# Norms with whole rows in freed buffers, low halves split by VectorE, and turned operands in a one-bank PSUM ring

## The chip, the cores and the metric

One core of a Trainium2 chip runs the whole kernel. The metric is the device time of one execution in microseconds (us), as the median of several runs. Five engines have instruction streams of their own: TensorE (PE, with its weight loads PEld), VectorE (DVE), ScalarE (ACT), GpSimd (POOL) and SyncE (SP), which here only issues transfers; "SPq" and "ACTq" are the queues of transfers that SyncE and ScalarE issue.

## What is computed

One decoder layer on x of 2048 tokens by 1024 features, all in float32:

```python
hn = rms_norm(h, mix_pre_g)
proj = hn @ w_in                       # q (512), k (128), v (128), conv input u (1024)
attn_out = sliding_window_attention(q, k, v, attn_sinks, rel_bias)   # window 128, 8 heads
conv_out = conformer_conv(u, ...)      # GLU, 31 causal taps, LayerNorm, silu, @ w_conv_pw
mixed = concatenate([attn_out, conv_out]) @ w_out
h = h + rms_norm(mixed, mix_post_g)
hn = rms_norm(h, ffn_pre_g)
f = (silu(hn @ w_gate) * (hn @ w_up)) @ w_down      # d_ff 2816
h = h + rms_norm(f, ffn_post_g)
```

The change concerns the two norms in the middle (behind `mixed` and ahead of the feed-forward products), and some splits of weights.

## The kernel before, in words

A float32 product is made of three matmuls: each operand is split into a high half (ScalarE's rounding copy, L127 for weights) and a low half (the difference, L129 for weights, by GpSimd if `on_pool`, else by VectorE). VectorE's operations go through the helpers `stt`, `vtt` and `vts`, so most of them show as L94, and TensorE's products as L85. The names in the profile are tile@stage: `w@A` is a weight tile of stage A. Tiles live in rings, where a new tile waits for the last reader of the tile that had the buffer before. The rings that matter here have in SBUF x 4, wx 1, gb 2, hl 8, ql 4, chl 5, mid 4, fa 4, at 2, fc 3, raw 2 and w 6 buffers, and in PSUM (banks of 128x512) mm 4, tr 3 and ct 1.

The tokens go in four tiles of 512. The stages are:

- A: the input projection of a tile. Its weights are loaded as raw@A (L137), or their low halves as w@A<-lo_in (L126) where an earlier tile has made them. A turned v goes over fa@A (copied by ScalarE, L398, then transposed, L407).
- B: sliding-window attention, in the tr ring, with masks on GpSimd (`affine_select`, L494).
- C: the convolution. Its 31 taps are multiply-adds of VectorE (fc@C<-glu@C,colt,fc@C) that run at a low priority beside everything up to about 1300 us; its tail transposes in the ct ring (L549, L601) and writes mixT to DRAM.
- U: `stage_fold` (L611) multiplies w_conv_pw into the convolution's half of w_out once, ahead of W0. Its splits are 4 in the ring mid and 8 in chl, and their 12 low halves are made by GpSimd.
- W0 to W3: `stage_w` (L706), the output projection of one tile. Its activations are loaded from mixT (L717), split (L719), and multiplied into the accumulators x@W (W0) or mid@W. W0 makes the low halves of w_out's attention rows (8, on GpSimd) and stores them; W1 to W3 load them.
- `norm_w` (L759), called N0 to N3 here, behind each W: the rows of the post-norm are loaded as two halves gb@W (L697); sums of squares by ScalarE (L765); an inverse root (`rsqrt`, L145 to L156, whose refinements are on GpSimd for W0 to W2); the accumulators are scaled as eight halves; x is loaded in part whole in wx (L778) and in part as halves in fa or at (L784), and added (L779, L785: for W0 the tile in wx and two halves on GpSimd, the others on VectorE; for W1 to W3 all on VectorE); the sum is stored to h_scr (L786), its squares are summed (L787), a second inverse root follows, and the scaled rows go to hn_scr.
- H: the feed-forward input is read back from hn_scr by columns and turned (`turned`, L827, in tr), scaled (L847), split and kept as operands. The first pair of tiles (H0) and the second pair (H2) are apart.
- F: the gate and up products (with raw@F loads at L914, kept partial sums gb@F<-keeps at L921, put into banks by ScalarE at L936), for two tiles at a time. G: the down projection, which reads fa@G<-mids (L1146), mb@G<-td (L1150), copies p@G (L1218) into banks (L1219). TS makes sums of w_down beforehand.

Stages are generators that yield a cost. Main stages run in a fixed sequence; the others sit in lanes (L1290 on) that are advanced by the main stage's yielded cost times a rate, so that a changed yield moves instructions of other stages too. A scheduler then fixes one order of instructions for each engine. Within an engine (and in SyncE's queue of transfers) an instruction that waits holds all that stand behind it.

The lines of `norm_w` that the prediction speaks of, cut:

```python
gb = load_gb(0)                                   # two halves in gb
...
post_scale(acc[s], gb, r[:, s : s + 1])           # two stt of 512 columns
...
(vtt if w in WV or w == 0 and s % 2 else ptt)(acc[s][:, cs], xt, acc[s][:, cs], ALU.add)
```

Of the kernel before, what the change touches and what calls it, by code (L numbers as in the profile page):

```python
# [37 lines left out]
def layer_kernel(ctx, tc, x, xT, cols, rows, sinks, relb, onehot, w_in, w_pw, w_out, w_gate, w_up, w_down, out):  # L38
# [572 lines left out]
    def stage_fold():  # L611
# [8 lines left out]
        for i in range(2):  # L620
            lab[0] = "U0"
            raw = two(w_pw[2 * i : 2 * i + 2].rearrange("c p t -> p c t"))
            wp += [split_w(raw[:, j], "mid") for j in range(2)]
            yield 2.76
        for n in range(2):
            wo = []
            for i in range(2):
                lab[0] = "U0"
                c = 4 + 2 * i
                raw = two(w_out[c : c + 2, :, n * T : (n + 1) * T].rearrange("c p t -> p c t"))  # L630
                wo += [split_w(raw[:, j], "chl") for j in range(2)]
                yield 0.1 if n else 2.76
# [60 lines left out]
    def load_gb(row):  # L693
        gb = []
        for n in range(2):
            t = f2("gb")
            nc.sync.dma_start(t, rows[row, n * T : (n + 1) * T].partition_broadcast(P))  # L697
            gb.append(t)
        return gb

    def post_scale(acc, gb, r):
        for n in range(2):
            cs = slice(n * T, (n + 1) * T)
            stt(acc[:, cs], acc[:, cs], r, gb[n], ALU.mult, ALU.mult)

    def stage_w(w, spill, atag, htags, mtag, bank_of, norm=None, ready=None):  # L706
# [17 lines left out]
        def weights(gi, n):  # L724
            ws = []
            for c in range(G * gi, G * gi + G, 2):
                if c < 4:
                    ws += weight(w_out[c : c + 2, :, n * T : (n + 1) * T].rearrange("c p t -> p c t"), lo_out[n, c : c + 2], w > 0)
# [7 lines left out]
        if G == 4:  # L736
            yield W_LEAD
# [15 lines left out]
        tail = norm_w(w, spill, acc, mtag)  # L753
# [5 lines left out]
    def norm_w(w, spill, acc, mtag):  # L759
        L = f"W{w}"  # L760
        lab[0] = L
        gb = load_gb(0)
        ssq = sm(4)
        for s in range(4):
            act(junk, acc[s], AF.Square, accum_out=ssq[:, s : s + 1])  # L765
            yield 0.5
            lab[0] = L
        r = rsqrt(ssq, 4, D, w < 3)
        yield 3
        lab[0] = L  # L770
        ssq2 = sm(4)
        for s in range(4):
            lab[0] = L
            post_scale(acc[s], gb, r[:, s : s + 1])
            r0 = w * T + s * P
            if s == (2 if mtag == "fa" else 0):
                xt = f4("wx")
                nc.sync.dma_start(xt, x[r0 : r0 + P])  # L778
                (vtt if w in WV else ptt)(acc[s], xt, acc[s], ALU.add)  # L779
            else:  # L780
                for n in range(2):
                    cs = slice(n * T, (n + 1) * T)
                    xt = f2(mtag if s == 1 or w > 1 else "fa")
                    nc.sync.dma_start(xt, x[r0 : r0 + P, cs])  # L784
                    (vtt if w in WV or w == 0 and s % 2 else ptt)(acc[s][:, cs], xt, acc[s][:, cs], ALU.add)  # L785
            nc.sync.dma_start(h_scr[r0 : r0 + P], acc[s])  # L786
            act(junk, acc[s], AF.Square, accum_out=ssq2[:, s : s + 1])  # L787
            yield 1.5
# [3 lines left out]
        lab[0] = L  # L792
        for s in range(4):
            act(acc[s], acc[s], AF.Copy, scale=r2[:, s : s + 1])
            if spill:
                r0 = w * T + s * P
                nc.scalar.dma_start(hn_scr[r0 : r0 + P], acc[s])
        yield 0.1
        hns[w] = acc

    hns = {}
# [39 lines left out]
    def stage_h_plain(ws, ops, n, off):  # L841
        L = f"H{ws[0]}"
        for k in range(4):
            lab[0] = L
            b = turned(ws[0], k + off, tr, COLTAG[ws[0]][k] if ws[0] else "fa")
# [501 lines left out]
    WV = [1, 2, 3]  # L1347
# [28 lines left out]
    lw.add("W0", stage_w(0, True, "x", ["hl"] * 4, "fa", mm), lambda: "A3" in started and "C0" in ld.done and "U" in lu.done)  # L1376
# [52 lines left out]
    run(stage_w(1, True, "mid", ["hl", "chl"], "at", mm, norm=lambda g: lh.add("N1", g), ready=lambda: stage_pre(ws, ops, mids[0], keeps[0], 0, Q0)))  # L1429
# [11 lines left out]
    lw.add("W2", stage_w(2, True, "mid", ["ql", "chl"], "at", tr))  # L1441
    lw.add("C3", stage_tail(3), lambda: since(lc, "T3", CS))
    lw.add("W3", stage_w(3, True, "mid", ["ql", "chl"], "at", tr, norm=lambda g: lw.add("N3", g)))
# [72 lines left out]
```

## Time and profile before

| | |
|---|---|
| median of 3 runs | 2044.41 us (2039.39 to 2044.48) |
| profiled execution, its own time | 2052.75 us |
| its span | 2051.0 us |
| TensorE busy | 1956.7 us, 95% of the span |
| VectorE busy | 1471.4 us, 72% |
| ScalarE busy | 953.2 us, 46% |
| GpSimd busy | 367.8 us, 18% |
| mean granted TensorE clock | 0.981 of full speed |
| moved by transfers | 454.57 MB, 222 GB/s |

The span is the time from the first to the last recorded instruction; the execution's own time holds 1.75 us more. A row of a timeline gives the start in us, the duration in us, the engine, the line, the operation, the tile written and the tiles read, the shape, the count of merged instructions, and in brackets the idle time of the engine before it with what ended that. "[6.75 <-issue]" means that the profile shows no releaser. In a row of waits stand the total in us, the number of times and the longest. A window row has after the bounds the length, the busy time and count of PE, PEld, DVE, ACT and POOL, the granted TensorE clock, the busy share of the transfer engines, and GB/s.

### The profile page before, as it was taken

How to read it: one execution, taken by the hardware profiler on the slowest of the kernel's cores; microseconds unless marked ns; L12 is line 12 of the kernel's file. 1: busy time of each engine (PE TensorE's matmuls, PEld its weight loads, DVE VectorE, ACT ScalarE, POOL GpSimd, SP SyncE). 2: the span in 40 equal slices, each digit the busy share in tenths (PEclk: the TensorE clock that was granted, in tenths of full speed). 3: DMA queues.
4: the chain of work that ended last, by engine and by line, in shares of the span. 5: the costliest groups of instructions: out<-in, count | busy, mean ns of one | idle time of the engine just before them, and what ended most of it. 6: DMA issues, size and time to landing. Idle time of an engine off the chain costs nothing.

```text
span 2051.0 us, 26796 instructions
## 1 busy us (share of the span) xinstructions
PE 1956.7 (95%) x8730; PEld 1556.6 (76%) x8730; DVE 1471.4 (72%) x2583; ACT 953.2 (46%) x1878; POOL 367.8 (18%) x438
## 2 busy tenths in 40 slices
PE   8999998998988899899999989999999999999997
PEld 6777776676756778678878777777878888888886
DVE  4999979967656789788748973678466665545557
ACT  5355354445736634333336454574544434345443
POOL 4012232114011300000000010035323323221003
PEclk9999999999999999999999999999999999999999
DMA  8787655458758875886467787697954443266654
GB/s 301 250 308 237 202 199 184 161 190 267 250 176 280 277 269 196 279 289 202 154 221 240 242 303 232 212 325 242 311 184 153 160 167 113 99 225 225 203 188 148
DMA packets 232028, 454.57 MB, mean 222 GB/s; under 512 B 23208, under 2 KB 48976, under 8 KB 231888
## 3 DMA queue, kind: packets, MB, share of 16 engines
q1 hardware_dynamic: 213648, 426.64, 61.9%
q10 hardware_dynamic: 18240, 26.22, 3.5%
q8 instruction: 69, 1.13, 0.2%
q14 instruction: 71, 0.58, 0.1%
HBM read 331.65 MB, written 121.12 MB: 221 GB/s over the span
## 4 chain that ended last, share of the span: by engine, by line
PE 59%; DMA 16%; DVE 15%; issue 4%; ACT 3%; POOL 2%; SPq 1%; DVEq 0%; ACTq 0%; POOLq 0%
PE mm@F L85 28%; PE mm@G L85 11%; PE mm@A L85 9%; DVE fc@C L94 5%; PE mm@W L85 4%; PE tr@B L85 3%; PE tr@W L85 2%; DVE hl@G L94 2%; DMA mixT<-fc@C 2%; DMA at@W<-mixT 1%; DMA gb@F<-keeps 1%; DVE mid@W L94 1%; DVE w@F L94 1%; DMA td<-fc@G 1%; DVE sm@G L94 1%
## 5 line engine op out<-in xcount | busy, mean ns | idle before, releaser
L94 DVE SCALAR_TENSOR_TENSOR fc@C<-glu@C,colt,fc@C 128x512 f32<-128x512 f32 x480 | 370.6, 790 | 2.6
L85 PE MATMUL mm@F<-hl@H,w@F 128*128 128x512 f32 x1056 | 258.4, 394 | 12.0 <-ACT mm@F L936 10.3
L85 PE MATMUL mm@G<-hl@G,hl@G 128*128 128x512 f32 x924 | 236.0, 395 | 9.8 <-ACT mm@G L1219 3.9
L85 PEld LDWEIGHTS mm@F<-hl@H,w@F 128*128 128x128 f32 x1056 | 199.5, 190 | 57.5 <-ACT mm@F L936 13.5
L85 PE MATMUL mm@A<-hl@A,w@A 128*128 128x512 f32 x840 | 212.5, 400 | 5.1 <-ACT w@A L127 2.4
L85 PEld LDWEIGHTS mm@G<-hl@G,hl@G 128*128 128x128 f32 x924 | 173.4, 190 | 48.4 <-DVE hl@G L94 4.6
L85 PE MATMUL mm@G<-w@G,hl@G 128*128 128x512 f32 x876 | 199.4, 389 | 0.0
L809 ACT ACTIVATE w@F<-chl@F 128x512 fp32r<-128x512 f32 x220 | 134.8, 624 | 129.6 <-PE mm@F L85 122.8
L85 PEld LDWEIGHTS mm@A<-hl@A,w@A 128*128 128x128 f32 x840 | 158.3, 191 | 43.2 <-ACT w@A L127 3.0
L85 PEld LDWEIGHTS mm@G<-w@G,hl@G 128*128 128x128 f32 x876 | 164.4, 188 | 34.2
L94 DVE TENSOR_TENSOR w@F<-chl@F,w@F 128x512 fp32r<-128x512 f32 x198 | 145.0, 734 | 38.6 <-ACT w@F L809 38.3
L85 PE MATMUL mm@F<-ql@H,w@F 128*128 128x512 f32 x528 | 131.5, 397 | 13.6 <-ACT mm@F L1043 5.6
L85 PE MATMUL mm@F<-mid@H,w@F 128*128 128x512 f32 x528 | 132.6, 397 | 0.9 <-DVE fa@F L94 0.3
L85 PE MATMUL mm@F<-p@H,w@F 128*128 128x512 f32 x528 | 130.0, 391 | 0.0
L85 PEld LDWEIGHTS mm@F<-ql@H,w@F 128*128 128x128 f32 x528 | 100.2, 191 | 37.2 <-ACT mm@F L1043 6.6
L85 PE MATMUL mm@F<-x@H,w@F 128*128 128x512 f32 x528 | 127.0, 391 | 0.8 <-ACT fa@F L958 0.8
L85 PEld LDWEIGHTS mm@F<-mid@H,w@F 128*128 128x128 f32 x528 | 100.4, 191 | 23.9 <-ACT mm@F L936 1.1
L85 PEld LDWEIGHTS mm@F<-p@H,w@F 128*128 128x128 f32 x528 | 100.0, 189 | 21.0
L85 PEld LDWEIGHTS mm@F<-x@H,w@F 128*128 128x128 f32 x528 | 98.4, 188 | 22.5 <-ACT fa@F L958 1.3
L127 ACT ACTIVATE w@A<-raw@A 128x512 fp32r<-128x512 f32 x110 | 67.5, 626 | 96.8 <-PE mm@A L85 63.6
L494 POOL TENSOR_SCALAR_AFFINE_SELECT p@B<-p@B 128x512 f32<-128x512 f32 x62 | 51.6, 843 | 278.0 <-ACT p@B L492 276.5
L94 DVE TENSOR_TENSOR w@G<-raw@G,w@G 128x512 fp32r<-128x512 f32 x73 | 52.5, 719 | 67.3 <-ACT w@G L809 66.3
(303 smaller groups left out, 3365.3 us busy)
## 6 DMA issues: line engine op xcount, KB each, us to landing
mids<-fa@F SPq DMA_DIRECT2D x154, 256.0 KB, 2.6
raw@A<-w_in SPq DMA_DIRECT2D x55, 512.0 KB, 4.6
w@A<-lo_in SPq DMA_DIRECT2D x84, 256.0 KB, 3.7
fc@G<-mids SPq DMA_DIRECT2D x77, 256.0 KB, 3.4
fa@G<-mids SPq DMA_DIRECT2D x75, 256.0 KB, 5.0
gb@F<-keeps SPq DMA_DIRECT2D x72, 256.0 KB, 4.2
w@W<-fold SPq DMA_DIRECT2D x32, 512.0 KB, 5.6
chl@F<-w_gate SPq DMA_DIRECT2D x22, 512.0 KB, 3.8
```

Source lines behind the costliest of these rows:

```text
L85: r = nc.tensor.matmul(*args, **kw)
L94: r = op(*args, **kw)
L127: act(w[:, 0], raw, AF.Copy)
L494: nc.gpsimd.affine_select(out=pg[:, kb].rearrange("p (i q) -> p i q", q=P), in_=pg[:, 1].rearrange("p (i q) -> p i q", q=P), compare_op=AL ...
L809: act(w[:, 0], x, AF.Copy)
```

## The change

Five edits go together:

1. `stage_fold` makes its 12 low halves, and W0 its 8, on VectorE (`on_pool=False`).
2. `norm_w` loads the rows as one whole 128x1024 tile and x as four whole tiles, all five in the ring chl, ahead of the scalings. It scales with four whole operations instead of eight halves, and adds with four whole ones, all on VectorE. The second scaling writes into the x tiles, from which hn_scr is stored. Its yields are changed, and the lists and arguments that it no longer needs are gone.
3. W0 yields W_LEAD (4.0) after its first activations, as W1 to W3 did.
4. `turned` for the first pair's plain operands (H0) writes in the ct ring (one bank) instead of tr.
5. hn_scr is stored after each row's scaling, with a yield between.

```diff
--- before.py
+++ after.py
@@ -620,7 +620,7 @@
         for i in range(2):
             lab[0] = "U0"
             raw = two(w_pw[2 * i : 2 * i + 2].rearrange("c p t -> p c t"))
-            wp += [split_w(raw[:, j], "mid") for j in range(2)]
+            wp += [split_w(raw[:, j], "mid", on_pool=False) for j in range(2)]
             yield 2.76
         for n in range(2):
             wo = []
@@ -628,7 +628,7 @@
                 lab[0] = "U0"
                 c = 4 + 2 * i
                 raw = two(w_out[c : c + 2, :, n * T : (n + 1) * T].rearrange("c p t -> p c t"))
-                wo += [split_w(raw[:, j], "chl") for j in range(2)]
+                wo += [split_w(raw[:, j], "chl", on_pool=False) for j in range(2)]
                 yield 0.1 if n else 2.76
             for m in range(4):
                 lab[0] = "U0"
@@ -690,20 +690,7 @@
                 vtt(acc[i][:, cs], acc[i][:, cs], o, ALU.add)
             yield 0.65 * len(units)
 
-    def load_gb(row):
-        gb = []
-        for n in range(2):
-            t = f2("gb")
-            nc.sync.dma_start(t, rows[row, n * T : (n + 1) * T].partition_broadcast(P))
-            gb.append(t)
-        return gb
-
-    def post_scale(acc, gb, r):
-        for n in range(2):
-            cs = slice(n * T, (n + 1) * T)
-            stt(acc[:, cs], acc[:, cs], r, gb[n], ALU.mult, ALU.mult)
-
-    def stage_w(w, spill, atag, htags, mtag, bank_of, norm=None, ready=None):
+    def stage_w(w, atag, htags, mtag, bank_of, norm=None, ready=None):
         G = KC // len(htags)
         L = f"W{w}"
         lab[0] = L
@@ -725,7 +712,7 @@
             ws = []
             for c in range(G * gi, G * gi + G, 2):
                 if c < 4:
-                    ws += weight(w_out[c : c + 2, :, n * T : (n + 1) * T].rearrange("c p t -> p c t"), lo_out[n, c : c + 2], w > 0)
+                    ws += weight(w_out[c : c + 2, :, n * T : (n + 1) * T].rearrange("c p t -> p c t"), lo_out[n, c : c + 2], w > 0, on_pool=False)
                 else:
                     for j in range(2):
                         ws.append(hl("w"))
@@ -733,8 +720,7 @@
             return ws
 
         nxt = acts(0)
-        if G == 4:
-            yield W_LEAD
+        yield W_LEAD
         for gi in range(KC // G):
             aa = nxt
             for n in range(2):
@@ -750,55 +736,50 @@
                         lab[0] = L
                         nxt = acts(gi + 1)
                     yield c
-        tail = norm_w(w, spill, acc, mtag)
+        tail = norm_w(w, acc)
         if norm:
             norm(tail)
         else:
             yield from tail
 
-    def norm_w(w, spill, acc, mtag):
+    def norm_w(w, acc):
         L = f"W{w}"
         lab[0] = L
-        gb = load_gb(0)
+
+        def whole(src):
+            t = f4("chl")
+            nc.sync.dma_start(t, src)
+            return t
+
+        gb = whole(rows[0].partition_broadcast(P))
         ssq = sm(4)
         for s in range(4):
             act(junk, acc[s], AF.Square, accum_out=ssq[:, s : s + 1])
-            yield 0.5
+            yield 0.75
             lab[0] = L
         r = rsqrt(ssq, 4, D, w < 3)
+        xs = [whole(x[w * T + s * P : w * T + (s + 1) * P]) for s in range(4)]
+        ssq2 = sm(4)
         yield 3
-        lab[0] = L
-        ssq2 = sm(4)
         for s in range(4):
             lab[0] = L
-            post_scale(acc[s], gb, r[:, s : s + 1])
+            stt(acc[s], acc[s], r[:, s : s + 1], gb, ALU.mult, ALU.mult)
+            yield 1.25
+            lab[0] = L
+            vtt(acc[s], xs[s], acc[s], ALU.add)
             r0 = w * T + s * P
-            if s == (2 if mtag == "fa" else 0):
-                xt = f4("wx")
-                nc.sync.dma_start(xt, x[r0 : r0 + P])
-                (vtt if w in WV else ptt)(acc[s], xt, acc[s], ALU.add)
-            else:
-                for n in range(2):
-                    cs = slice(n * T, (n + 1) * T)
-                    xt = f2(mtag if s == 1 or w > 1 else "fa")
-                    nc.sync.dma_start(xt, x[r0 : r0 + P, cs])
-                    (vtt if w in WV or w == 0 and s % 2 else ptt)(acc[s][:, cs], xt, acc[s][:, cs], ALU.add)
             nc.sync.dma_start(h_scr[r0 : r0 + P], acc[s])
             act(junk, acc[s], AF.Square, accum_out=ssq2[:, s : s + 1])
-            yield 1.5
+            yield 1.25
         lab[0] = L
         r2 = rsqrt(ssq2, 4, D, w < 3)
         yield 3
-        lab[0] = L
         for s in range(4):
-            act(acc[s], acc[s], AF.Copy, scale=r2[:, s : s + 1])
-            if spill:
-                r0 = w * T + s * P
-                nc.scalar.dma_start(hn_scr[r0 : r0 + P], acc[s])
-        yield 0.1
-        hns[w] = acc
-
-    hns = {}
+            lab[0] = L
+            act(xs[s], acc[s], AF.Copy, scale=r2[:, s : s + 1])
+            r0 = w * T + s * P
+            nc.scalar.dma_start(hn_scr[r0 : r0 + P], xs[s])
+            yield 1.25
 
     def load_cols(w, k, tag):
         t = f2(tag, (P, 4, P))
@@ -842,7 +823,7 @@
         L = f"H{ws[0]}"
         for k in range(4):
             lab[0] = L
-            b = turned(ws[0], k + off, tr, COLTAG[ws[0]][k] if ws[0] else "fa")
+            b = turned(ws[0], k + off, tr if ws[0] else ct, COLTAG[ws[0]][k] if ws[0] else "fa")
             u = f2("gb")
             act(u, b, AF.Copy, scale=g_ffn[:, k + off : k + off + 1])
             nc.scalar.dma_start(hT[ws[0] // 2][k + off], u)
@@ -1344,7 +1325,6 @@
     PRES = {0: 20, 2: 16}
     Q0 = 8
     POOL_LO = (3, 6)
-    WV = [1, 2, 3]
     PRE_S0, PRE_S2 = 22, 16
     H1, H2, H3, H4 = 0, 4, 7, 11
     lb = Lane(RB, 0)
@@ -1373,7 +1353,7 @@
 
     lb.add("X", stage_x(), lambda: "x1" in started)
     lu.add("U", stage_fold(), lambda: "A2" in started)
-    lw.add("W0", stage_w(0, True, "x", ["hl"] * 4, "fa", mm), lambda: "A3" in started and "C0" in ld.done and "U" in lu.done)
+    lw.add("W0", stage_w(0, "x", ["hl"] * 4, "fa", mm), lambda: "A3" in started and "C0" in ld.done and "U" in lu.done)
     TGA = [["hl"] * 8, ["mid"] * 4 + ["chl"] * 4, ["hl"] * 8, ["mid"] * 4 + ["hl"] * 4]
     xa = {}
     warm = mm()
@@ -1426,7 +1406,7 @@
     ws, ops = (0, 1), {}
     for n, off in (("B11", 0), ("B21", 4)):
         lh.add(n + ".0", stage_h_plain(ws, ops, n, off))
-    run(stage_w(1, True, "mid", ["hl", "chl"], "at", mm, norm=lambda g: lh.add("N1", g), ready=lambda: stage_pre(ws, ops, mids[0], keeps[0], 0, Q0)))
+    run(stage_w(1, "mid", ["hl", "chl"], "at", mm, norm=lambda g: lh.add("N1", g), ready=lambda: stage_pre(ws, ops, mids[0], keeps[0], 0, Q0)))
     lc.hold = lambda: "S0" not in lh.done
     lh.until("B21.0")
     lh.add("S0", stage_h_sums(ws, ops), lambda: f"P0.{PRE_S0}" in started and "B3" in lb.done)
@@ -1438,9 +1418,9 @@
     lc.rates["T3"] = RC3
     ws, ops = (2, 3), {}
     lw.add("C2", stage_tail(2))
-    lw.add("W2", stage_w(2, True, "mid", ["ql", "chl"], "at", tr))
+    lw.add("W2", stage_w(2, "mid", ["ql", "chl"], "at", tr))
     lw.add("C3", stage_tail(3), lambda: since(lc, "T3", CS))
-    lw.add("W3", stage_w(3, True, "mid", ["ql", "chl"], "at", tr, norm=lambda g: lw.add("N3", g)))
+    lw.add("W3", stage_w(3, "mid", ["ql", "chl"], "at", tr, norm=lambda g: lw.add("N3", g)))
     lw.add("B11.2", stage_h_plain(ws, ops, "B11", 0))
     run(stage_p2((0, 1), mids[0], td))
     lw.until("N3")
```

The rows of x and of the post-norm weights now share chl with U's weights, W's second activations, and F's raw weights. What moves, in the fixed orders:

On SyncE at W0's start, the transfers around W0's first activations (fa@W<-mixT) and the weights of A3 (w@A, raw@A). Before:

```order
L131 DMA lo_out<-w@W_593_3644 128x512
L137 DMA raw@W_616_3775<-w_out 128x2x512
L126 DMA w@A_605_3695<-lo_in 128x512
L126 DMA w@A_606_3698<-lo_in 128x512
L717 DMA fa@W_576_3576<-mixT 128x512
L717 DMA fa@W_578_3581<-mixT 128x512
```

Of the change:

```order
L126 DMA w@A_595_3651<-lo_in 128x512
L131 DMA lo_out<-w@W_582_3592 128x512
L137 DMA raw@W_609_3733<-w_out 128x2x512
L126 DMA w@A_596_3654<-lo_in 128x512
L137 DMA raw@A_618_3778<-w_in 128x1024
L704 DMA fa@W_576_3576<-mixT 128x512
L704 DMA fa@W_578_3581<-mixT 128x512
```

The activations now stand behind other weights of A3 than before, whose buffers have readers some 50 matmuls earlier, and one raw load lies between.

On VectorE at N0, from the first scaling on (ql@A and vtok are A3's results for attention, fc@C the taps). Before, with the last of the eight scalings first:

```order
L94 SCALAR_TENSOR_TENSOR x@W_573_3573<-x@W_573_3573,sm@W_728_4416,gb@W_725_4408 128x512
L94 SCALAR_TENSOR_TENSOR fc@C_705_4284<-glu@C_704_4282,colt,fc@C_705_4284 128x512
L94 TENSOR_TENSOR x@W_573_3573<-fa@W_745_4521,x@W_573_3573 128x512
L94 TENSOR_TENSOR x@W_575_3575<-fa@W_748_4538,x@W_575_3575 128x512
L94 TENSOR_TENSOR x@W_573_3573<-fa@W_746_4524,x@W_573_3573 128x512
L94 SCALAR_TENSOR_TENSOR fc@C_705_4284<-glu@C_704_4282,colt,fc@C_705_4284 128x512
L94 SCALAR_TENSOR_TENSOR ql@A_763_4650<-mm@A_761_4618,ql@A_763_4650 128x512
```

Of the change, with all four scalings:

```order
L94 SCALAR_TENSOR_TENSOR x@W_572_3572<-x@W_572_3572,sm@W_739_4489,chl@W_736_4481 128x1024
L94 SCALAR_TENSOR_TENSOR x@W_574_3574<-x@W_574_3574,sm@W_739_4489,chl@W_736_4481 128x1024
L94 SCALAR_TENSOR_TENSOR x@W_573_3573<-x@W_573_3573,sm@W_739_4489,chl@W_736_4481 128x1024
L94 SCALAR_TENSOR_TENSOR x@W_575_3575<-x@W_575_3575,sm@W_739_4489,chl@W_736_4481 128x1024
L94 TENSOR_TENSOR x@W_572_3572<-chl@W_741_4506,x@W_572_3572 128x1024
L94 TENSOR_TENSOR x@W_574_3574<-chl@W_743_4510,x@W_574_3574 128x1024
L94 SCALAR_TENSOR_TENSOR fc@C_590_3634<-fc@C_589_3632,fc@C_590_3634 128x512
L94 SCALAR_TENSOR_TENSOR ql@A_756_4602<-mm@A_754_4570,ql@A_756_4602 128x512
L94 TENSOR_TENSOR x@W_573_3573<-chl@W_742_4508,x@W_573_3573 128x1024
L410 COPY vtok<-mm@A_755_4595 128x512
```

The halves from fa are gone, and the additions that GpSimd made now stand here.

On SyncE at N3, the row and x loads between the down projection's (fa@G<-mids, mb@G<-td). Before:

```order
L784 DMA at@W_1967_11650<-x 128x512
L1150 DMA mb@G_1971_11673<-td 128x512
L1146 DMA fa@G_1982_11747<-mids_4773 128x512
L697 DMA gb@W_1951_11574<-rows 128x512
L1150 DMA mb@G_1983_11749<-td 128x512 x2
L1146 DMA fa@G_1988_11780<-mids_4773 128x512
L1146 DMA fa@G_1991_11800<-mids_4773 128x512
L697 DMA gb@W_1952_11576<-rows 128x512
```

Of the change, where the row stands 14 transfers ahead of this piece:

```order
L751 DMA chl@W_1947_11568<-x 128x1024
L751 DMA chl@W_1948_11570<-x 128x1024
L751 DMA chl@W_1949_11572<-x 128x1024
L1127 DMA fa@G_1963_11664<-mids_4758 128x512
L751 DMA chl@W_1950_11574<-x 128x1024
L786 DMA fc@H_2079_12369<-hn_scr 128x4x128
```

The four tiles of x, 512 KB each, stand almost together, and the row comes well before them.

## The prediction

> **What bounds the kernel now.** First the page's busy times.
>
> ```profile
> PE 1956.7 (95%) x8730; PEld 1556.6 (76%) x8730; DVE 1471.4 (72%) x2583; ACT 953.2 (46%) x1878; POOL 367.8 (18%) x438
> ```
>
> TensorE (PE) is busy for 1956.7 of 2051.0 us, so it sits idle for 94.3 us. The change leaves every matmul in place, so it can gain only from that idle time, and from matmuls that run at a reduced clock. Second, the windows by stage show where the two are.
>
> ```profile
> core 0: us, PE busy (x) PEld busy (x) DVE busy (x) ACT busy (x) POOL busy (x), PEclk, DMA share, GB/s
> 250.00:520.00 270.00, 256.46 (x1160) 187.29 (x1159) 214.39 (x444) 128.66 (x300) 66.73 (x95) 0.96 0.62 204
> 520.00:750.00 230.00, 211.54 (x956) 158.94 (x955) 160.58 (x311) 125.15 (x266) 35.99 (x52) 0.97 0.74 248
> 1050.00:1500.00 450.00, 423.88 (x1865) 343.69 (x1864) 310.64 (x514) 240.00 (x436) 84.86 (x113) 0.98 0.78 265
> ```
>
> W0 with its norm lies in the first of these (13.5 us of idle), W1 with its norm in the second (18.5), W2 and W3 with theirs in the third (26.1). Third, what ended TensorE's idle times: from 300 to 520 us, and from 600 to 1500 us.
>
> ```profile
> PE mm@W L85 <- ACT hl@W L719: 5.1, 1, 5.1
> PE mm@A L407 <- ACT fa@A L398: 4.5, 1, 4.5
> PE mm@W L85 <- ACT x@W L688: 2.0, 1, 2.0
> ...
> PE mm@F L85 <- ACT mm@F L936: 10.6, 9, 1.9
> ...
> PE mm@G L85 <- ACT mm@G L1219: 3.9, 1, 3.9
> ```
>
> The first and third are W0's start, the second W0's norm; the last two stand beside the norms of W1 (N1) and W3 (N3). These are the places to follow.
>
> **W0's norm (the largest term).** From the timeline by engine, 480 to 500 us:
>
> ```profile
> 480.54 10.02 DVE L94 SCALAR_TENSOR_TENSOR x@W<-x@W,sm@W,gb@W 128x512 f32<-128x512 f32 x8
> 481.37 1.72 POOL L785 TENSOR_TENSOR x@W<-fa@W,x@W 128x512 f32<-128x512 f32 x1 [0.87 <-DVE x@W L94]
> 483.05 4.20 POOL L494 TENSOR_SCALAR_AFFINE_SELECT p@B<-p@B 128x512 f32<-128x512 f32 x4
> 487.22 2.79 POOL L779 TENSOR_TENSOR x@W<-wx@W,x@W 128x1024 f32<-128x1024 f32 x1
> 487.30 1.94 PE L85 MATMUL tr@B<-p@B,vtok 128*64 128x512 f32 x8 [1.69 <-POOL p@B L494]
> 493.51 0.60 ACT L398 ACTIVATE fa@A<-mm@A 128x512 f32<-128x512 f32 x1 [6.75 <-issue]
> 494.16 1.11 PE L407 MATMUL mm@A<-ident,fa@A 128*128 128x128 f32 x4 [4.49 <-ACT fa@A L398]
> 479.99 2.90 PE L85 MATMUL mm@A<-mid@A,w@A 128*128 128x512 f32 x12
> 494.93 5.28 PE L85 MATMUL mm@A<-mid@A,w@A 128*128 128x512 f32 x12
> 632.56 5.39 DVE L94 SCALAR_TENSOR_TENSOR mid@W<-mid@W,sm@W,gb@W 128x512 f32<-128x512 f32 x8 [2.60 <-POOL sm@W L156]
> 638.47 1.22 DVE L94 TENSOR_TENSOR mid@W<-wx@W,mid@W 128x1024 f32<-128x1024 f32 x1
> ```
>
> ScalarE's copy fa@A needs an fa buffer; the profile names no releaser (6.75 <-issue), but the four buffers hold the halves of x that the slow additions have yet to read, so I read the wait as one for that ring. Behind the copy TensorE waits 4.49 us, then runs twelve matmuls at half clock: 5.28 instead of 2.90, another 2.38. Ahead of it the masks on GpSimd (POOL) cost 1.69. Together 8.56 us. The eight scalings take 10.02 beside GpSimd's work and 5.39 without it (the same block at W1).
>
> In the changed kernel the norm touches neither fa nor GpSimd's adder. The trace has no 128x1024 scaling; four of them are bounded by 5.39 (eight halves back to back) and 8 x 0.75 = 6.0 (a single half, by the taps' row further down). All additions on VectorE (DVE) are 4 x 1.22 = 4.9 us. The block that a mm@A eviction can stand behind is then four scalings and two additions, 7.8 to 8.4 us, against 12 us. **I take 7 of the 8.56**; bounds 3 (the block delays an eviction by about what a mask did, and the half clock remains) and 8.56.
>
> **W0's start.** The queue of SyncE (SP), then TensorE and ScalarE:
>
> ```profile
> 348.81 3.55 SPq L126 DMA_DIRECT2D w@A<-lo_in  x2
> 352.41 0.90 SPq L717 DMA_DIRECT2D fa@W<-mixT  x2
> 357.44 0.63 ACT L719 ACTIVATE hl@W<-fa@W 128x512 fp32r<-128x512 f32 x1 [3.97 <-DMA fa@W<-mixT]
> 358.12 7.25 PE L85 MATMUL mm@W<-w@W,hl@W 128*128 128x512 f32 x20 [5.08 <-ACT hl@W L719]
> ```
>
> Two loads of w@A hold the queue for 3.55 us, until their buffers' last readers have run; W0's first columns of mixT stand behind them, and 5.08 us of TensorE behind those. Twenty matmuls then take 7.25; at 2.90 per twelve they would take 4.83, so the low clock costs 2.42. By the order, the loads ahead of fa@W now wait for buffers that are read some 50 matmuls earlier; 50 x 0.242 = 12 us is more than the 5.08. One load of raw@A, whose buffer comes free once those weights are split, still stands between. **I take 5 of the 7.50** (5.08 + 2.42), bounds 0 and 7.5; the 2.0 behind ScalarE's x@W copy stays, since that is the eviction of a bank.
>
> The Trainium skill, "TensorE: Matmul & The Clock Gate", section "Part 1: The HAM clock gate (the "warmup" mystery)", says that the array falls to half clock after about 3.4 us without work, and recovers after as long a busy time. Both places above agree (4.49 and 5.08 us of idle, slow matmuls behind); by that rule, leaving 2 us of the 5.08 would still give 3.08 + 2.42 = 5.5 here.
>
> **The twenty low halves (U, W0).** From the groups between 250 and 480 us (the taps' group is that between 1084 and 1165, where GpSimd is idle; behind the first bar stand busy us and mean ns), the timeline, and a window:
>
> ```profile
> L129 POOL TENSOR_TENSOR w@W<-raw@W,w@W 128x512 fp32r<-128x512 f32 x8 | 12.7, 1587 | 45.5 <-ACT w@W L127 45.4
> L94 DVE SCALAR_TENSOR_TENSOR fc@C<-glu@C,colt,fc@C 128x512 f32<-128x512 f32 x59 | 42.9, 748 | 0.4
> L94 DVE TENSOR_TENSOR hl@W<-fa@W,hl@W 128x512 fp32r<-128x512 f32 x8 | 5.5, 688 | 5.0 <-ACT hl@W L719 5.0
> 336.75 3.88 POOL L129 TENSOR_TENSOR w@W<-raw@W,w@W 128x512 fp32r<-128x512 f32 x2 [3.25 <-ACT w@W L127]
> 337.71 3.47 DVE L94 SCALAR_TENSOR_TENSOR fc@C<-glu@C,colt,fc@C 128x512 f32<-128x512 f32 x2
> 400.00:430.00 30.00, 30.00 (x138) 21.84 (x136) 28.96 (x64) 8.51 (x26) 3.08 (x4) 1.00 0.60 200
> ```
>
> On VectorE a half is 0.69 us: 20 x 0.69 = 13.8 us added. Each one on GpSimd lengthens what VectorE does beside it: two taps took 3.47 instead of 2 x 0.75, so some 1.0 us per subtraction, 20 us in all. VectorE is thus relieved by about 6 us, with bounds of 13.8 more work (nothing beside it) and 6 less. It is nearly full up to 430 us, but TensorE has no idle there outside the places already counted: **0**. If taps are delayed, C1's tail comes later.
>
> The Trainium skill, "SBUF — State Buffer", section "Who interferes with whom", has the port pair of VectorE and GpSimd as an exclusive lock held for a whole instruction. By it each tap could be held up for a whole 1.59 us, and the relief would be 20 x 1.59 - 13.8 = 18 us; the row above shows about 1.0, so the measurement decides.
>
> **N1, N2, N3.** Additions were on VectorE already; what changes is where rows and x come from. The windows around them, the wait behind N1's mm@F, then the timeline:
>
> ```profile
> 640.00:720.00 80.00, 68.81 (x301) 54.05 (x300) 50.91 (x69) 53.12 (x93) 20.17 (x24) 0.98 0.90 305
> 1170.00:1220.00 50.00, 44.36 (x199) 35.69 (x198) 44.69 (x76) 27.34 (x50) 9.24 (x22) 1.00 0.83 285
> ACT mm@F L936 <- DMA gb@F<-keeps: 7.4, 5, 2.5
> 1323.54 2.74 DVE L94 SCALAR_TENSOR_TENSOR mid@W<-mid@W,sm@W,gb@W 128x512 f32<-128x512 f32 x4 [3.08 <-DMA gb@W<-rows]
> 1329.38 15.99 PE L85 MATMUL mm@G<-hl@G,hl@G 128*128 128x512 f32 x61 [3.94 <-ACT mm@G L1219]
> 1179.35 0.38 SPq L1146 DMA_DIRECT2D fa@G<-mids  x1
> 1188.98 0.32 SPq L786 DMA_DIRECT2D h_scr<-mid@W  x1
> ```
>
> At N3 VectorE's scalings wait 3.08 us for gb, a copy p@G behind them is late, and TensorE waits 3.94. With the row already there this goes, and I take **3** (0 to 4). At N2 a store of h holds SyncE's queue from 1179.7 to 1189, with fa@G and mb@G behind it; now the x loads don't alternate with the stores, but the four scalings still block, so I take **2** of the 5.6 us of idle (0 to 4). At N1 the stretch is short of transfers (DMA 0.90) and of the 10.6 us that TensorE waits for mm@F the copies behind it waited 7.4 for gb@F<-keeps between 640 and 720. With gb free of W's rows those loads can be issued earlier; where transfers are the bound this helps only in part, and I take **2** (0 to 4).
>
> Against that stands an unseen cost: x now comes as four 512 KB loads issued together. 2 MB at 305 GB/s is 6.9 us, ahead of raw@F, fa@G and mb@G on the same queue. Bounds: nothing, or 6.9 at each of three norms, 20.7. The same 2 MB passed before too, in pieces, so most of it is paid already; I take nearer to the lower end, a fifth of the upper one, **4**.
>
> **Turned operands in ct.** The trace has the same step for the second pair:
>
> ```profile
> 1324.84 0.60 PE L827 MATMUL tr@H<-ident,fc@H 128*128 128x128 f32 x4
> 1326.37 0.69 ACT L847 ACTIVATE gb@H<-tr@H,colt 128x512 f32<-128x512 f32 x1
> ```
>
> With one bank, a tile's four transposes (0.60) wait for ScalarE's copy of the tile before (0.69). In the new order eight tiles stand 20 matmuls or more apart, 20 x 0.242 = 4.8 us, which hides the copy: **0**. Without this cover it is 8 x 0.69 = 5.5 worse; and as attention keeps the three tr banks to itself, up to the same 5.5 better.
>
> **Sum.** 7 + 5 + 0 + 3 + 2 + 2 - 4 = 15 us. The profiled execution took 2052.75 us (span 2051.0 and 1.75 around it), so it would come to 2037.75; that is 8.3 above the median of 2044.41, and by the same amount below, the forecast is **2029.4 us**.
>
> **Rivals.** (1) *Only W0 gains* (chance 0.20): N1 to N3 give nothing, because those stretches are filled by VectorE and transfers, the burst of x takes its 4, and W0's start gains half. 7 + 2.5 - 4 = 5.5, about 2039. For it: VectorE 44.69 of 50 us at N2, DMA 0.90 at N1. Against: TensorE's 3.94 hang on one late row.
>
> (2) *The bursts of x cost more than W0 gains* (0.17): on SyncE the loads wait for chl buffers, which W's last products release, and raw@F, fa@G and mb@G stand behind them. At the full 6.9 us for N1, N2 and N3, 20.7 less 12 for W0 is 8.7 slower, about 2053; with some of N1 to N3's gains, 2050. It decides where a load that TensorE needs is issued within 6.9 us behind the burst. For it: DMA 0.83 and 0.90, so the transfers have little room. Against: by the new order the first fa@G behind N3's burst is needed some 60 matmuls later, 60 x 0.242 = 15 us.
>
> (3) *The change does not relieve* (0.09): the 6.75 us before fa@A was not the fa ring, or the whole scalings hold up evictions as long as GpSimd did. Then W0's norm gives its lower bound 3, its start 0 and the rest cancels: about 2042 to 2046.
>
> **How the numbers follow.** The forecast has 0.54, with its own range of 2014 to 2038: from all places whole (8.56 + 7.5 + 12 = 28, 2016, and a little from tr) to half of the sum. The rivals have 0.20, 0.17 and 0.09. About 0.3%, 6.1 us, is what a measurement here can tell from no change: faster is below 2038.3, slower above 2050.5. Faster are the forecast and half of rival 1, 0.64. Slower are 0.14 of rival 2 and a third of rival 3, 0.17. The rest, 0.19, is the same. The range, 2014 to 2053, reaches to the middle of rival 2.
>
> **What would show it.** After the change: no GpSimd additions in W0's norm, its scaling block under 6.5 us and no idle of 4.5 us before L407's transposes; the first mm@W without a 5 us wait; no gb wait at N3. If SyncE's queue shows long holds at the x loads with raw@F or fa@G landing late, rival 2 holds. What would make the sum wrong is a wait that the old order did not have, at attention's last tile or at C1's tail, since no row of before shows it.

## The result and the profile after

| | before | changed |
|---|---|---|
| median | 2044.45 us (2039.39 to 2046.85, 4 runs) | 2019.21 us (2014.80 to 2022.36, 4 runs) |
| ratio to before | | 0.987, 95% interval 0.9839 to 0.9901 |
| span of the profiled execution | 2051.0 us | 2013.1 us |
| mean granted clock | 0.981 | 0.987 |

The change is 25 us faster, where 15 were forecast. The ratios, here and below, compare undisturbed executions; one of the four of u3 below took 5043.64 us and is left out of its ratio. The two profiled executions differ by 38, more than the medians: before's, at 2052.75, was slower than all its timed ones and the change's was its fastest, so differences between these two are read with a control (c0 below, the kernel before profiled again). The page's busy times of the changed kernel:

```profile
PE 1941.8 (96%) x8730; PEld 1549.1 (77%) x8730; DVE 1455.3 (72%) x2578; ACT 953.1 (47%) x1878; POOL 333.8 (17%) x415
```

TensorE's idle time fell from 94.3 to 71.3 us, and its busy time by 15, with the same 8730 matmuls: fewer of them ran at a low clock. What TensorE waited for from 300 to 520 us, where before had 5.1, 4.5, 2.0 and 1.7:

```profile
PE mm@W L85 <- ACT hl@W L706: 1.4, 2, 1.0
PE mm@W L85 <- ACT x@W L688: 0.2, 1, 0.2
```

Both places of W0 are free. At W0's start, SyncE and then TensorE:

```profile
336.03 0.33 SPq L137 DMA_DIRECT2D raw@A<-w_in  x1
336.42 0.92 SPq L704 DMA_DIRECT2D fa@W<-mixT  x2
344.28 0.32 SPq L131 DMA_DIRECT2D lo_out<-w@W  x1
...
346.16 0.97 PE L85 MATMUL mm@W<-w@W,hl@W 128*128 128x512 f32 x3 [0.99 <-ACT hl@W L706]
```

The first activations are issued 9.7 us ahead of the first product; before it was 5.7. At W0's norm, the copy fa@A on ScalarE, the whole scalings and additions on VectorE, and the transposes behind the copy:

```profile
462.40 0.59 ACT L398 ACTIVATE fa@A<-mm@A 128x512 f32<-128x512 f32 x1
465.78 4.87 DVE L94 SCALAR_TENSOR_TENSOR x@W<-x@W,sm@W,chl@W 128x1024 f32<-128x1024 f32 x4 [3.55 <-POOL sm@W L156]
470.57 2.35 DVE L94 TENSOR_TENSOR x@W<-chl@W,x@W 128x1024 f32<-128x1024 f32 x2
467.89 0.27 PE L407 MATMUL mm@A<-ident,fa@A 128*128 128x128 f32 x1
```

The scalings took 4.87 instead of 10.02 us. But note the first row: fa@A now comes 3.4 us ahead of them, where before it came 13.0 us behind their start. The experiments turn on this row. Around N1, and from 1100 to 1420 us (N2, N3), TensorE waited for:

```profile
PE mm@F L85 <- ACT mm@F L917: 2.6, 3, 1.1
PE mm@F L85 <- DVE gb@F L94: 2.1, 1, 2.1
...
PE tr@H L808 <- ACT gb@H L828: 5.0, 1, 5.0
PE tr@W L85 <- ACT mid@W L688: 3.4, 1, 3.4
PE mm@F L85 <- DVE p@G L1160: 3.0, 1, 3.0
```

Around N1 the wait behind the kept sums (its copy is now L917) is 2.6; in the same stretch, 590 to 760 us, the kernel before had 10.3 in its first profile and 8.6 in c0. At N3 the wait of 3.9 for mm@G is gone, and one of 5.0 for the turned operands stands there instead.

### The profile page after: what moved, and what is told of

The parts are those of the page before. It is cut to its first block, busy times and chain, and to the rows that moved or that the text cites. A ratio compares the mean times of both kernels' runs of the same rounds, so it can differ in the third digit from the quotient of the medians.

```text
span 2013.1 us, 26722 instructions
## 1 busy us (share of the span) xinstructions
PE 1941.8 (96%) x8730; PEld 1549.1 (77%) x8730; DVE 1455.3 (72%) x2578; ACT 953.1 (47%) x1878; POOL 333.8 (17%) x415
## 4 chain that ended last, share of the span: by engine, by line
PE 43%; DMA 12%; DVE 7%; issue 3%; POOL 2%; ACT 2%; SPq 1%; ACTq 0%; DVEq 0%; POOLq 0%
PE mm@F L85 26%; PE mm@G L85 13%; PE tr@W L85 3%; DMA gb@F<-keeps 2%; DMA td<-fc@G 1%; DMA mids<-fa@F 1%; DMA wx@G<-h_scr 1%; DMA raw@F<-w_up 1%; DVE hl@G L94 1%; DMA at@W<-mixT 1%; DVE w@F L94 1%; DMA mixT<-fc@C 1%; DVE x@G L94 1%; DVE chl@F L94 1%; DMA chl@H<-hT 1%
## 5 line engine op out<-in xcount | busy, mean ns | idle before, releaser
L94 DVE SCALAR_TENSOR_TENSOR fc@C<-glu@C,colt,fc@C 128x512 f32<-128x512 f32 x480 | 355.3, 758 | 2.6
L85 PE MATMUL mm@G<-hl@G,hl@G 128*128 128x512 f32 x924 | 231.0, 395 | 2.4 <-ACT hl@G L790 1.7
```

What stands on the lines that cost most here:

```text
L85: r = nc.tensor.matmul(*args, **kw)
L94: r = op(*args, **kw)
```

## The experiments

The theory: the gain sits at W0's start (the place of fa@W in SyncE's queue), in W0's norm (GpSimd's additions and the fa ring) and at the other norms. Rivals: the relief of VectorE from GpSimd; attention's tr ring; or an order of instructions that any of the edits would have mended.

### Undoing one part each

`u1_low_on_gpsimd` drops `on_pool=False` in `stage_fold` and `stage_w`:

```diff
-            wp += [split_w(raw[:, j], "mid", on_pool=False) for j in range(2)]
+            wp += [split_w(raw[:, j], "mid") for j in range(2)]
```

> The changed kernel with one part undone: the 20 low halves of U and W0 on GpSimd again. My theory (the gain of 25 us sits at W0's start and in the norms) expects 0 to 3 us more than the changed kernel, 2019 to 2022: VectorE gains work back only where TensorE does not wait for it. The rival that the relief of VectorE from GpSimd carries the gain expects 10 us more or worse, 2029 and up, and in the profile a slower W0 start.

Measured: 2027.25 us, ratio to before 0.9898 (0.9873 to 0.9924): 8 us worse than the changed kernel by the medians and 6 to 8 by the ratios, with intervals that touch. The expectation of 0 to 3 was too small. One place is in SyncE's queue, in the waits between 340 and 356 us and the timeline:

```profile
SPq L131 <- POOL w@W L129: 4.3, 1, 4.3
...
350.81 0.32 SPq L131 DMA_DIRECT2D lo_out<-w@W  x1
351.18 1.75 SPq L704 DMA_DIRECT2D fa@W<-mixT  x2
356.33 1.65 PE L85 MATMUL mm@W<-w@W,hl@W 128*128 128x512 f32 x3 [3.66 <-ACT hl@W L706]
```

The store of a low half (lo_out<-w@W) waits 4.3 us for GpSimd to make it, and fa@W stands behind the store. With the halves on VectorE, the order has fa@W ahead of it. The place in the queue is what counts, not the engine's speed: in the changed kernel a store lo_out waits even longer, 6.9 us for VectorE, but behind fa@W. A second place lies earlier, in U, at attention's tile 0 (VectorE, GpSimd, then TensorE):

```profile
202.80 9.35 DVE L94 SCALAR_TENSOR_TENSOR fc@C<-glu@C,colt,fc@C 128x512 f32<-128x512 f32 x14
206.02 8.95 POOL L129 TENSOR_TENSOR chl@U<-wx@U,chl@U 128x512 fp32r<-128x512 f32 x2 [6.15 <-ACT chl@U L127]
214.93 4.19 POOL L494 TENSOR_SCALAR_AFFINE_SELECT p@B<-p@B 128x512 f32<-128x512 f32 x4
219.17 3.68 PE L85 MATMUL tr@B<-p@B,vtok 128*64 128x512 f32 x8 [6.36 <-POOL p@B L494]
```

Two of U's low halves take GpSimd 8.95 us beside a full VectorE, attention's masks stand behind them, and TensorE waits 6.36. In the kernel before it is the other engine that is held up at this place:

```profile
205.19 15.00 DVE L94 SCALAR_TENSOR_TENSOR fc@C<-glu@C,colt,fc@C 128x512 f32<-128x512 f32 x14
207.76 3.02 POOL L129 TENSOR_TENSOR chl@U<-wx@U,chl@U 128x512 fp32r<-128x512 f32 x2 [5.51 <-ACT chl@U L127]
228.82 1.28 PE L85 MATMUL tr@B<-kz,ql@A 64*128 64x256 f32 x12 [3.95 <-DVE sm@B L454]
```

The same two halves take GpSimd 3.02, the fourteen taps take VectorE 15.00 instead of 9.35, and TensorE waits 3.95 for attention's sm@B, which stands behind the taps. From 180 to 240 us TensorE idles 6.4 us in u1, 4.0 in before, and none in the changed kernel, d1 and p1, which all have the halves on VectorE. Here the rival, VectorE's relief from GpSimd, is right; the prediction had not counted this place.

`u2_no_lead`:

```diff
-        yield W_LEAD
+        if G == 4:
+            yield W_LEAD
```

> The changed kernel with one part undone: no W_LEAD ahead of W0's first weights. My theory expects W0's first activations to stand behind the loads of two late weights again, a wait of some 5 us before the first mm@W with slow matmuls behind: 7 to 12 us more than the changed kernel, 2026 to 2031. The rival that the freed buffers or the low halves ended that wait expects at most 2 us more, and no such wait in the profile.

Measured: 2015.88 us, ratio 0.9846 (0.9822 to 0.9869). The wait came back as expected, behind the two w@A loads:

```profile
342.49 3.58 SPq L126 DMA_DIRECT2D w@A<-lo_in  x2
346.11 1.83 SPq L704 DMA_DIRECT2D fa@W<-mixT  x2
350.48 3.52 PE L85 MATMUL mm@W<-w@W,hl@W 128*128 128x512 f32 x8 [3.86 <-ACT hl@W L706]
```

The time did not: it is the changed kernel's, within the intervals. So a stall that is plainly there is given back elsewhere; the table below says in part where.

`u3_turned_in_tr`:

```diff
-            b = turned(ws[0], k + off, tr if ws[0] else ct, ...)
+            b = turned(ws[0], k + off, tr, ...)
```

> The changed kernel with one part undone: the first pair's turned operands in the tr ring again. My theory expects no difference beyond 3 us either way, 2016 to 2022. The rival that attention's waits in the tr ring were what the change ended expects 5 to 10 us more, with waits of TensorE for tr@B or tr@H near 500 to 600 us.

Measured: 2020.34 us, ratio 0.9864 (0.9840 to 0.9888). As expected: taken out of the whole, this part costs nothing that can be measured.

`u4_norm_before` puts the former `norm_w`, `load_gb`, `post_scale` and `WV` back into the changed kernel, and with them the former stores of hn_scr (edits 2 and 5):

```diff
-            vtt(acc[s], xs[s], acc[s], ALU.add)
+            (vtt if w in WV or w == 0 and s % 2 else ptt)(acc[s][:, cs], xt, acc[s][:, cs], ALU.add)
```

> The changed kernel with one part undone: the norms as before (halves of x in fa, at and wx, rows in gb, GpSimd's additions in W0's norm, and its yields). My theory expects W0's norm to cost TensorE its 8.5 us again and the other norms 3 to 8: 2031 to 2036. The rival that the gain came from the order at W0's start alone expects 0 to 3 us more, 2019 to 2022.

Measured: 2020.2 us, ratio 0.9858 (0.9834 to 0.9881). My theory expected 12 to 17 us more and got about 1. The largest part of the diff, on which my largest term rested, isn't needed where the others are there.

### One part alone on the kernel before

The same edits the other way round, each alone on the kernel before.

> The kernel before with one part alone: the 20 low halves of U and W0 on VectorE. My theory expects 0 to 3 us less than before, 2041 to 2044. The rival that VectorE's relief carries the gain expects 10 us less or better; the rival that 13.8 us of added work delays the taps expects some us more.

> The kernel before with one part alone: W_LEAD ahead of W0's first weights. My theory expects the wait of 5.1 us before the first mm@W and the slow matmuls behind it to go, 5 to 12 us less than before, 2032 to 2039. The rival that it needs the freed buffers as well expects at most 2 us less, with a wait of several us before the first mm@W.

> The kernel before with one part alone: the first pair's turned operands in ct. My theory expects no difference beyond 3 us, 2041 to 2047. The rival that one bank stalls the turned operands or C1's tail expects 3 to 6 us more; the rival that the tr ring is what binds attention expects 5 us less.

> The kernel before with one part alone: the norms with whole rows in chl and no GpSimd additions. My theory expects the waits of 1.7 and 4.5 us and the slow matmuls of W0's norm to go and 3 to 8 us at the others, 10 to 17 us less than before, 2027 to 2034. The rival that the bursts of x cost as much as is gained expects at most 4 us less.

Measured, against 2046.07 us of before (27 runs):

| alone | median | ratio and interval |
|---|---|---|
| d1 low halves | 2037.10 us | 0.9956 (0.9939 to 0.9973) |
| d2 W_LEAD | 2031.46 us | 0.9924 (0.9900 to 0.9949) |
| d3 turned in ct | 2038.11 us | 0.9966 (0.9950 to 0.9981) |
| d4 norms | 2035.23 us | 0.9954 (0.9938 to 0.9970) |

My theory's numbers held for none: d2 gained more than its 5 to 12 us, d1 and d3 more than their 3, and d4 just missed its 10. For d1 and d3 the rivals' numbers (10 us from VectorE's relief, 5 from the tr ring) stand nearer. For d1 the rival is right in part: its profile has no wait behind VectorE in U, and VectorE's busy time is 1460.5 us against 1469.6 in c0, with twenty subtractions more. For d3 the place is another: its profile gains 3.2 us at N1 and nothing where attention waits in U. By the ratios the four are worth 9.0, 15.5, 7.0 and 9.4 us, together 41; the whole change gave 25. The parts overlap: several of them mend the same stall. In d2, with the norm as it was and GpSimd adding, ScalarE's copy and VectorE's scalings at W0's norm are:

```profile
469.30 0.60 ACT L398 ACTIVATE fa@A<-mm@A 128x512 f32<-128x512 f32 x1 [1.71 <-PE mm@A L85]
468.45 9.59 DVE L94 SCALAR_TENSOR_TENSOR x@W<-x@W,sm@W,gb@W 128x512 f32<-128x512 f32 x8 [0.65 <-POOL sm@W L156]
```

The scalings are as slow as ever (9.59), but fa@A comes 0.85 us behind their start, and TensorE does not wait. In d4, with the new norm and the old start of W0, it is the same (fa@A 1.15 us behind the start):

```profile
472.79 5.99 DVE L94 SCALAR_TENSOR_TENSOR x@W<-x@W,sm@W,chl@W 128x1024 f32<-128x1024 f32 x4
473.94 0.59 ACT L398 ACTIVATE fa@A<-mm@A 128x512 f32<-128x512 f32 x1
```

So with either edit A3's copy no longer waits for a half of x. That made a revised theory, and the last four runs.

### The revised theory: W0 needs the lead and the low halves, and the place of fa@A

The theory is that W0's start needs both, and that the lead alone takes A3's copy out of the norm's way. `p1_lead_and_low` is the kernel before with d1's and d2's edits. `m2_n0_adds_on_vector` is the kernel before with one list changed:

```diff
-    WV = [1, 2, 3]
+    WV = [0, 1, 2, 3]
```

`c0_before_again` and `c1_after_again` are the two kernels unchanged, as controls.

> The kernel before with two parts: W_LEAD ahead of W0's weights and the 20 low halves on VectorE; norms and the turned operands as before. My revised theory: W0's start needs both, and W0's norm is mended by W_LEAD alone, since it moves the norm away from A3's fa@A; so nearly the whole gain, 18 to 26 us less than before, 2020 to 2028, with less than 3.5 us of wait before the first mm@W and none before L407. The rival that the norm's new buffers carry a part of their own leaves it 8 us or more behind the changed kernel, 2027 and up.

> The kernel before with all additions of W0's norm on VectorE, rows and x in their old buffers. If GpSimd's additions hold the fa buffers that A3's fa@A waits for, the waits of 1.7 and 4.5 us and the slow matmuls behind them go: 5 to 9 us less than before, 2037 to 2041. The rival that the ring itself, or the scalings, hold fa@A leaves most of the 4.5 us and gives at most 2 us.

> The kernel before, unchanged, profiled a second time as a control. Both theories expect the same waits (5.1 us before the first mm@W, 4.5 us before L407 behind fa@A) and a time of 2040 to 2052; how far its times at equal matmul counts stand from the first profile says how large a difference between two profiles must be.

> The changed kernel, unchanged, as a control beside the next two: 2015 to 2022 again. If the runs without W_LEAD or with the norms of before (2016 and 2020) were really as fast, this stays within 5 us of them; the rival is that the changed kernel was measured too slow in its first four runs, and then it comes out at 2012 or less.

Measured against 2045.65 us of before (17 runs): p1 2022.5 us, ratio 0.9876 (0.9857 to 0.9895), so two small edits bring 23 us; c1 2019.1 us, ratio 0.9858 (0.9838 to 0.9879), 27 us, as in the first measurement and not below the runs without a part. That is what the theory expected of p1, and so are its rows (VectorE, ScalarE, TensorE):

```profile
457.92 11.07 DVE L94 SCALAR_TENSOR_TENSOR x@W<-x@W,sm@W,gb@W 128x512 f32<-128x512 f32 x8 [3.40 <-POOL sm@W L156]
459.86 0.60 ACT L398 ACTIVATE fa@A<-mm@A 128x512 f32<-128x512 f32 x1 [0.89 <-PE mm@A L85]
346.15 0.96 PE L85 MATMUL mm@W<-w@W,hl@W 128*128 128x512 f32 x3 [1.02 <-ACT hl@W L719]
```

The scalings take 11.07 us, longer than the 10.02 of before, and TensorE has no wait behind fa@A. c0's one run took 2041.96 us, with the same waits of 4.9 and 4.5. In c0 the profile also names the releaser that it had left open:

```profile
491.47 0.60 ACT L398 ACTIVATE fa@A<-mm@A 128x512 f32<-128x512 f32 x1 [7.07 <-DVE x@W L94]
492.12 1.11 PE L407 MATMUL mm@A<-ident,fa@A 128*128 128x128 f32 x4 [4.49 <-ACT fa@A L398]
```

It is an addition of x@W on VectorE, which reads a half of x out of the fa ring. m2 took 2048.93 us, ratio 1.0014 (0.9998 to 1.0029): no gain, where the view that GpSimd's additions are the price expected 5 to 9 us. VectorE, ScalarE and TensorE at its norm:

```profile
480.85 6.89 DVE L94 SCALAR_TENSOR_TENSOR x@W<-x@W,sm@W,gb@W 128x512 f32<-128x512 f32 x8
491.37 1.06 ACT L787 ACTIVATE junk<-x@W 128x1024 bf16<-128x1024 f32 x1 [3.75 <-DVE x@W L94]
492.43 0.58 ACT L398 ACTIVATE fa@A<-mm@A 128x512 f32<-128x512 f32 x1
493.26 0.58 PE L85 MATMUL tr@B<-kz,ql@A 64*128 64x256 f32 x2 [5.85 <-DVE ql@A L94]
```

Without GpSimd's additions the scalings take 6.89 instead of 10.02, yet the additions themselves now stand on VectorE ahead of ql@A, and the wait of 4.5 has become one of 5.85. Here fa@A stands behind a sum of squares on ScalarE, which waits for VectorE in turn. At W0's norm m2's profile is 2.0 us faster than c0; it loses 2.5 in U and 4.5 at N1, far from its edit.

### Where the time is, at equal matmuls

All kernels run the same 8730 matmuls, so the times at which the matmul of the same number starts can be compared. The table has the change of that time over a stretch of matmuls, against c0, in us; minus is faster. "Elsewhere" is the rest of the whole.

| kernel | U (750 to 1500) | W0's start (1500 to 1750) | W0's norm (2000 to 2250) | N1 (2750 to 3250) | N2, N3 (4750 to 6000) | elsewhere | whole |
|---|---|---|---|---|---|---|---|
| before, first profile | 0.0 | +0.3 | -0.2 | +1.2 | +3.0 | +6.6 | +10.7 |
| changed | -1.6 | -13.8 | -9.7 | -6.6 | +3.0 | +1.5 | -27.2 |
| changed, again | -2.2 | -13.8 | -9.7 | -6.4 | +3.3 | -0.3 | -29.0 |
| p1 lead, low | -4.3 | -12.4 | -7.4 | -1.9 | +1.0 | +6.9 | -18.1 |
| m2 | +2.5 | -0.3 | -2.0 | +4.5 | +0.5 | +1.9 | +7.1 |
| u1 no low | +2.1 | -5.8 | -9.1 | -3.4 | +4.8 | -6.2 | -17.5 |
| u2 no lead | +1.4 | -5.0 | -6.6 | -7.3 | -1.7 | -9.2 | -28.3 |
| u3 no ct | -2.7 | -13.8 | -9.7 | -1.2 | +7.3 | -1.8 | -21.8 |
| u4 no norms | -4.3 | -12.4 | -7.3 | -2.7 | +0.6 | +4.2 | -21.8 |
| d1 low | -3.4 | -3.3 | -4.6 | +0.8 | +3.0 | +3.5 | -4.1 |
| d2 lead | +0.1 | -7.3 | -9.0 | +0.2 | +0.6 | -3.5 | -18.9 |
| d3 ct | +1.2 | -1.1 | +0.4 | -3.2 | +0.6 | -1.4 | -3.3 |
| d4 norms | -0.1 | -3.4 | -9.0 | -0.9 | +3.5 | -2.9 | -12.8 |

Each row is one profile, and a column holds idle time, a lower clock and a little of another order of long and short matmuls. The first row shows how far two profiles of one kernel stand apart: up to 1.2 us in four columns, 3.0 at N2 and N3, and 10.7 in all. U falls with the low halves, but for u2. W0's start falls by 12 to 14 where lead and low halves are both there, and by at most 7.3 elsewhere. W0's norm falls by 7 to 10 with the lead or with the norms, whichever, and by 4.6 with the low halves alone. N1 gives its 6 to 7 only in the changed kernel and in u2.

What the 13.8 at W0's start consist of is seen in the windows from 340 to 375 us, of c0 and of the changed kernel:

```profile
340.00:375.00 35.00, 28.14 (x108) 20.52 (x109) 32.12 (x74) 12.30 (x34) 4.39 (x3) 0.80 0.58 181
340.00:375.00 35.00, 33.76 (x173) 26.30 (x171) 33.34 (x86) 16.56 (x42) 1.54 (x2) 1.00 0.65 208
```

TensorE's idle time fell from 6.9 to 1.2 us, and a granted clock of 0.80, which costs some 7 of 35 us, became 1.00. More than half of that stall's price was clock.

Against the changed kernel u2 lacks 9 us at W0's start, 3 in U and 3 at W0's norm, and wins 5 back at N2 and N3 and 11 elsewhere. Of these 11, some 4 lie at W1's start (matmuls 2250 to 2750), where the changed kernel, from 520 to 632 us, has a wait for W1's first activations that u2 does not have and that was 1.2 us in before:

```profile
PE mm@W L85 <- ACT chl@W L706: 4.4, 1, 4.4
```

The rest is spread, and why N2 and N3 go better in u2 isn't settled.

At N3 of the changed kernel a stall was replaced. VectorE, ScalarE and TensorE there:

```profile
1280.23 4.88 DVE L94 SCALAR_TENSOR_TENSOR mid@W<-mid@W,sm@W,chl@W 128x1024 f32<-128x1024 f32 x4
1288.50 0.68 DVE L94 TENSOR_TENSOR ql@H<-gb@H,ql@H 128x512 fp32r<-128x512 f32 x1
1288.81 1.04 ACT L772 ACTIVATE junk<-mid@W 128x1024 bf16<-128x1024 f32 x1
1289.85 0.67 ACT L828 ACTIVATE gb@H<-tr@H,colt 128x512 f32<-128x512 f32 x1
1290.57 1.12 PE L808 MATMUL tr@H<-ident,at@H 128*128 128x128 f32 x4 [4.97 <-ACT gb@H L828]
```

The row is there in time, so the scalings no longer wait for it. But the second pair's turned tiles come in a bunch, and the last one needs a tr bank, which the copy gb@H frees. That copy needs a buffer that the low half ql@H reads, and the low half stands behind the 4.88 us of scalings; but it is done at 1289.18. ScalarE, on which the copy stands, has no idle time from 1285.15 on: four splits of G and two of the norm's sums of squares (L772) run ahead of the copy. So its place in ScalarE's order held it last.

## Why the prediction was right, and where its steps were not

The direction and the range held, and so did three of the places: the changed kernel is faster because TensorE's waits at W0's start, W0's norm and N1 went. The size was 15 against 25. That the time fell in the range is in part luck: the edit behind the largest term isn't needed where the others are there (u4), an edit priced at nothing is (u1), and terms that were too small stand beside gains that did not come (N2, N3). Term by term, in the changed kernel against c0:

- **W0's start, 5, bounds 0 to 7.5**: 13.8, beyond the bounds. The cause, fa@W behind two late w@A loads, is shown (u2 brings it back). Mis-sized, for three reasons. The clock was priced at 2.42, for the twenty matmuls behind the wait; it cost some 7. I left 2.0 behind x@W as staying, and it fell to 0.2. And I read it as a gain of the lead alone. The lead alone swaps the w@A loads for a store lo_out that waits for GpSimd (3.67 us of wait before the first mm@W remain in d2, 3.66 in u1), and only with the low halves on VectorE does fa@W come ahead of that store too.
- **W0's norm, 7, bounds 3 to 8.56**: 9.7, in both profiles. Right that fa@A waited for a half of x in the fa ring: c0 names the releaser, an addition on VectorE. Not borne out that GpSimd's additions were the price: m2 takes them away and wins at most 2.0 there, and p1 keeps them and has no wait. What decides is whether A3's fa@A has to wait for a half of x, and the lead ends that as well as the new buffers do (d2, d4, p1, u4).
- **The twenty low halves, 0**: the step that failed. Undone they cost 6 to 8 us, alone they give 9. The relief of VectorE was seen (6 us; 9 in d1's profile), but my windows began at 250 us, while U's halves run from 191 to 295. So I missed TensorE's 3.95 us behind VectorE at 229, and on SyncE the store of a half that holds fa@W.
- **Turned operands in ct, 0, bounds -5.5 to 5.5**: about 1 in the whole, and 7 by itself (0.9966), of which its profile shows 3.2 at N1. The cause is not shown. No wait for the one bank is seen in the changed kernel.
- **N1, 2, bounds 0 to 4**: 6.6, since more than the rows in gb acted there: without the ct ring 1.2, without the norms 2.7 and without the low halves 3.4 are left, and alone only the ct ring gives anything clear of the 1.2 between two profiles. How the parts share N1 stays open. The 10.6 us that I set beside N1 are those of 600 to 1500 us; N1's own were 10.3, and 8.6 in c0.
- **N2 and N3, 3 + 2**: 3.0 worse, as much as c0 and the first profile differ there, so no gain is shown. The wait for the row went as foreseen, and the turned operands' wait of 5.0 took its place.
- **The burst of x, -4**: not seen. No wait of TensorE in the changed kernel names a late raw@F, fa@G or mb@G. At N2 the x loads did hold SyncE's queue for 5.2 us, until chl buffers came free, but TensorE has no wait from 1045 to 1179 us. Rival 2 is not borne out; W0's two terms alone are larger than it.

What the prediction missed as a whole is that its terms are not additive. The four parts alone would make 41 us. The stalls of before hung on a few places in fixed orders, and several edits each move the same instruction past the same obstacle. And as it warned, there is a wait that the old order did not have, though at another place than it named: 4.4 us at W1's start.

The half clock behind a long wait was rightly foreseen: after 3.86 us of idle in u2, eight matmuls took 3.52 us, 440 ns each, against 242 elsewhere. The Trainium skill, "TensorE: Matmul & The Clock Gate", section "Part 1: The HAM clock gate (the "warmup" mystery)", states half clock after about 3.4 us without work, and this trace agrees there. But it is not all of the clock's price at W0's start. In c0 the granted clock is 0.52 from 354.6 to 361.4 us, behind the wait of 4.9, and also 0.54 from 344.3 to 347.7, with no idle time ahead of it in the profile, and from 368.2 to 371.6, behind 1.96 us of it. A sum that counts only the matmuls right behind a long wait is too small here.

## What to carry to other kernels

In kernels whose queues run in a fixed order, ask of a stall which single instruction is late and what stands ahead of it on its own queue, a store that waits for another engine included; the load of an engine alone says less. Before a large rewrite, try the smallest edit that moves that instruction: here two small ones (a yield, and the engine of some subtractions) bring 23 of the 27 us measured beside them. And measure each part both alone and left out, since parts that mend the same stall look useful alone and useless when undone.

## What the runs showed of the hardware that was not expected

A whole 128x1024 scaling took 1.28 us (1278 ns in the mean over twelve), below twice the 0.67 that halves take back to back, which I had as the lower bound. GpSimd's three additions lengthened the block of eight scalings by 10.02 - 6.89 = 3.1 us (before against m2, with masks beside it in both), while 1.72 + 2.79 + 0.6 = 5.1 us of them lay beside it: about 0.6 us of VectorE per us of GpSimd, by this estimate. Which engine pays can change between kernels with the same instructions at a place: in U the two halves took GpSimd 3.02 us and the fourteen taps VectorE 15.00 in before, and 8.95 and 9.35 in u1. The Trainium skill, "SBUF — State Buffer", section "Who interferes with whom", describes a lock under which the later one waits for a whole instruction: GpSimd's 8.95 fits a series of such waits, while at W0's norm VectorE lost less than the whole overlap.
